# A gated FFN on one core: sixteen of its 22 up chunks by seven products of block sums, and the down projection cut into six parts

## The chip, the cores and the metric

The kernel runs on one core of one Trainium2 chip. Its engines work side by side, each through its own queue of instructions in a fixed order: PE (matmuls, with PEld for the loading of weights), ACT (activations and copies), DVE (elementwise work on vectors), POOL (GpSimd) and SP, which issues most DMAs. The metric is the time of one execution on the device, in microseconds (us), as the median of several runs.

## The reference

An encoder of two layers on 512 tokens of width 1024. Layer 0 mixes tokens by gated linear attention in both directions, layer 1 by grouped-query softmax attention; both end in the same kind of FFN, which is what changes here:

```
def conv_ffn(h, w_up, w_conv, b_conv, w_down):
    u = h @ w_up                                  # 512 x 1024 by 1024 x 5632
    u = conv over 3 neighbouring tokens of each feature + b_conv
    val, gate = jnp.split(u, 2, axis=-1)          # 2816 features each
    return (jax.nn.silu(gate) * val) @ w_down     # 512 x 2816 by 2816 x 1024

x = x + conv_ffn(rmsnorm(x, norm_ffn[i]), ...)
```

All inputs are float32.

## The kernel before

Features lie on the 128 partitions and the 512 tokens along the free axis (S = 512, P = 128). x is held as eight tiles x[0] to x[7] of 128 x 512.

**Precision by two pieces.** A matmul operand is split into a high part, rounded to fp32r by ACT (L143), and a low part, the rest, by DVE (L144). A product of two such operands is three matmuls: high by high, high by low, low by high (mm3, L268 to L272). Each matmul has weights of 128 x 128 and streams 512 columns into one bank of PSUM.

**Weights.** The class Weights holds a list of things to make, in the order in which they are used. half() makes what is wanted, if it isn't there yet, and one piece more. A piece is half of a raw tile: 1 MB comes by DMA on SP's queue into one of two raw buffers, and each half (128 x 1024) becomes a pair wh, wl with three buffers each. For some attention weights the low part is made by ACT (L124) and an accumulating DMA on POOL's queue (L133) instead of DVE.

**Norm.** Norm.chunk(c) makes high and low parts of the weighted x[c] (tiles xhl, L235, L240) and sums squares (L244, L248). The 1/rms of each token is applied late: tokens() forms it by small matmuls (L256), DVE, a power on POOL (L204) and a copy (L260); rows() transposes it to a row layout R (L211, L266). The up products are multiplied by R as they leave PSUM (L605).

**FFN.** For each of 22 chunks of 128 features (FC = 22) the loop runs two tiles, t = 0 the value and t = 1 the gate, of 8 x 3 matmuls (feature_tile) in banks of the tags "acc" (three) and "s" (two). Then for each: times R (L605, DVE), the middle tap with bias (L607, ACT), the two outer taps (L608, L609, DVE); silu on the gate (L611, ACT), the product (L612, DVE), and its high and low parts gu (L614 ACT, L615 DVE), which stay in SBUF. When all 22 chunks are done, the down projection runs for each of eight output tiles over all 22 chunks, 66 matmuls into one bank, and adds the bank to x[c] (L633). In layer 0 Norm.chunk(c) of the next norm follows at once; in layer 1 the tile goes to the output (L637), and the last tile is handled in two halves of 256 columns (L640, L641).

**Order.** The program is written as a sequence of tiles and instructions. When it is built, a planner orders each engine's queue from that sequence and from what it expects to be ready, and puts in the waits for data and for buffers that are still in use. On the chip each queue runs in that order.

## Time and profile before

| | us |
|---|---|
| time of a run: median of 3 | 1134.56 |
| lowest and highest | 1133.87, 1135.52 |
| span of the profiled execution, from the first to the last instruction | 1132.5 |
| PE, DVE, ACT, POOL busy in the profiled execution | 1124.2, 683.7, 481.2, 86.2 |
| first FFN, about 237 to 532 us: PE, DVE busy | 295.0, 191.3 |
| attention, about 532 to 773 us: PE, DVE busy | 239.8, 145.2 |
| second FFN with the tail, about 773 to 1133 us: PE, DVE busy | 355.8, 202.4 |

The time of the profiled execution itself is known only as its span; the runs' median is 2.1 us above it, for what lies around the first and the last instruction. In the rows below, L12 is line 12 of the kernel before; a group reads "line engine operation out<-in, shapes xcount | busy us, mean ns | idle time before it and what ended it". Records of matmuls overlap, since they are pipelined: the distance from one start to the next is the time that a matmul costs in a row of them.

### The profile page before, as it was taken

The numbers are of one execution on the slowest core, as the hardware profiler recorded it, in microseconds if no ns is written. First come the engines' busy times: TensorE is split into PE (matmuls) and PEld (weight loads), VectorE is DVE, ScalarE is ACT, GpSimd is POOL, SyncE is SP. The second block draws the span as 40 slices with busy tenths as digits, with TensorE's granted clock in tenths as the row PEclk, the third lists the DMA queues.
The fourth block names the chain that finished last, engine by engine and source line by source line (L and its number), as shares of the span: only waits on it lengthen the run. The fifth ranks groups of instructions, "written<-read, shape, count | busy, mean of one in ns | idle before, by whom it ended". The sixth has DMA issues, their size and how long they took to land. (4 is left out here: it accounts for less than half of the span.)

```text
span 1132.5 us, 13117 instructions
## 1 busy us (share of the span) xinstructions
PE 1124.2 (99%) x5266; PEld 937.4 (83%) x5266; DVE 683.7 (60%) x989; ACT 481.2 (42%) x690; POOL 86.2 (8%) x74
## 2 busy tenths in 40 slices
PE   9999999999999999999999999999999999999998
PEld 7878888888888888888888888888888888888887
DVE  6576654577777777633325688766777677762221
ACT  5555233444444444422234667644444444442210
POOL 0214110000000000000004343000000000000000
PEclk9999999999999999999999999999999999999999
DMA  6322221222323223233247765423232232323320
GB/s 230 121 100 77 75 75 38 75 98 89 112 75 112 95 91 112 76 110 106 81 132 194 182 171 158 150 75 112 75 112 80 107 111 76 111 84 121 130 93 19
DMA packets 24589, 120.06 MB, mean 106 GB/s; under 512 B 2896, under 2 KB 3536, under 8 KB 13008
## 3 DMA queue, kind: packets, MB, share of 16 engines
q1 hardware_dynamic: 17328, 102.29, 26.0%
q0 software_dynamic: 2304, 8.39, 3.9%
q10 hardware_dynamic: 4896, 8.54, 2.1%
q8 instruction: 41, 0.67, 0.2%
q14 instruction: 20, 0.16, 0.0%
HBM read 100.34 MB, written 2.10 MB: 90 GB/s over the span
## 5 line engine op out<-in xcount | busy, mean ns | idle before, releaser
L143 ACT ACTIVATE wh<-raw 128x1024 fp32r<-128x1024 f32 x164 | 172.9, 1055 | 338.0 <-PE up L271 132.8
L144 DVE TENSOR_TENSOR wl<-raw,wh 128x1024 fp32r<-128x1024 f32 x164 | 203.8, 1243 | 142.7 <-ACT wh L143 142.3
L270 PE MATMUL up<-xhl,wh 128*128 128x512 f32 x704 | 274.3, 390 | 0.0
L272 PE MATMUL up<-xhl,wl 128*128 128x512 f32 x704 | 273.9, 389 | 0.0
L271 PE MATMUL up<-xhl,wh 128*128 128x512 f32 x704 | 273.9, 389 | 0.0
L271 PEld LDWEIGHTS up<-xhl,wh 128*128 128x128 f32 x704 | 132.2, 188 | 27.6
L272 PEld LDWEIGHTS up<-xhl,wl 128*128 128x128 f32 x704 | 132.1, 188 | 27.4
L270 PEld LDWEIGHTS up<-xhl,wh 128*128 128x128 f32 x704 | 132.1, 188 | 27.2
L271 PE MATMUL dn<-gu,wh 128*128 128x512 f32 x354 | 137.3, 388 | 0.0
L272 PE MATMUL dn<-gu,wl 128*128 128x512 f32 x354 | 137.3, 388 | 0.0
L270 PE MATMUL dn<-gu,wh 128*128 128x512 f32 x354 | 137.3, 388 | 0.0
L605 DVE TENSOR_TENSOR u<-up,R 128x512 f32<-128x512 f32 x88 | 60.3, 687 | 52.7 <-PE up L272 52.7
L299 PE MATMUL vg<-wh,xhl 128*128 128x512 f32 x256 | 80.1, 391 | 1.5 <-DVE halfneg L188 0.7
L607 ACT ACTIVATE y<-u,cw 128x512 f32<-128x512 f32 x88 | 71.1, 811 | 20.4 <-DVE u L605 20.4
L270 PEld LDWEIGHTS dn<-gu,wh 128*128 128x128 f32 x354 | 66.5, 188 | 13.8
L271 PEld LDWEIGHTS dn<-gu,wh 128*128 128x128 f32 x354 | 66.5, 188 | 13.7
L272 PEld LDWEIGHTS dn<-gu,wl 128*128 128x128 f32 x354 | 66.5, 188 | 13.5
L325 PE MATMUL op<-oT,wh 128*128 128x512 f32 x256 | 71.1, 394 | 0.3 <-DVE oT L710 0.3
L609 DVE SCALAR_TENSOR_TENSOR y<-u,cw,y 128x511 f32<-128x511 f32 x88 | 65.9, 751 | 2.9
L608 DVE SCALAR_TENSOR_TENSOR y<-u,cw,y 128x511 f32<-128x511 f32 x88 | 65.6, 746 | 0.6 <-ACT y L607 0.6
L611 ACT ACTIVATE y<-y 128x512 f32<-128x512 f32 x44 | 27.9, 633 | 87.8 <-DVE y L609 87.8
L299 PEld LDWEIGHTS vg<-wh,xhl 128*128 128x128 f32 x256 | 48.0, 188 | 12.4 <-DVE g L368 1.0
(187 smaller groups left out, 1432.3 us busy)
## 6 DMA issues: line engine op xcount, KB each, us to landing
raw<-in_w_up_dram SPq DMA_DIRECT2D x44, 1024.0 KB, 4.8
raw<-in_w_down_dram SPq DMA_DIRECT2D x22, 1024.0 KB, 4.8
wl<-raw POOLq DMA_DIRECT2D x16, 512.0 KB, 4.8
pr<-p ACTq DMA_DIRECT2D x32, 256.0 KB, 3.1
raw<-in_w_vg_dram SPq DMA_DIRECT2D x6, 1024.0 KB, 4.8
raw<-in_w_akq_dram SPq DMA_DIRECT2D x5, 1024.0 KB, 5.3
raw<-in_w_kq_dram SPq DMA_DIRECT2D x4, 1024.0 KB, 4.7
raw<-in_w_gout_dram SPq DMA_DIRECT2D x4, 1024.0 KB, 4.8
```

The lines of the kernel that those rows point to most:

```text
L143: act.activation(hi[:, sl], r[:, sl], AF.Copy)
L144: dve.tensor_tensor(lo[:, sl], r[:, sl], hi[:, sl].bitcast(F32), ALU.subtract)
L270: mm(ps, wh, mh, start=start, stop=False)
L271: mm(ps, wh, ml, start=False, stop=False)
L272: mm(ps, wl, mh, start=False, stop=stop)
L299: mm(ps[j][:, :width], hl[k][i == 2][:, js[j]], (wl if i == 1 else wh)[:, sl], start=k == 0 and i == 0, stop=k == KC - 1 and i == 2)
L325: mm(pss[ng][n], wt[:, sl], mv, start=k == 0 and i == 0, stop=k == KC - 1 and i == 2)
L605: dve.tensor_tensor(u, ps, norm.R, ALU.mult)
L607: act.activation(y, u, AF.Identity, scale=w(1), bias=w(3))
L608: dve.scalar_tensor_tensor(y[:, 1:], u[:, : S - 1], w(0), y[:, 1:], ALU.mult, ALU.add)
L609: dve.scalar_tensor_tensor(y[:, : S - 1], u[:, 1:], w(2), y[:, : S - 1], ALU.mult, ALU.add)
L611: act.activation(res[1], res[1], AF.Silu)
```

## The change

Chunks 0 to 5 of each layer (PLAIN = 6) stay as they were, in a new function plain(). For chunks 6 to 21 seven() computes the value and the gate tile by a scheme of seven block products. The input is cut into four blocks: 512 features (four k tiles) by 256 tokens (half of the columns). The weights of a chunk are four blocks too: value and gate by the two halves of the 1024 input features. Instead of eight block products (each 4 x 3 matmuls of 256 columns) there are seven, on sums and differences of blocks.

- build() makes the input's forms once for each layer, during the plain chunks 1 and on (STEPS steps after each tile): the normed input h with R already multiplied in (scaled input), the four sums T1 to T4, and high and low parts of the seven forms used. T3 and T4 are combined on POOL, the rest on DVE.
- rowA1, sum12, sum43 and oneA22 make the weights' forms for each chunk: four sums of 512 columns on DVE, and high and low parts of three pieces of 1024 and one of 512.
- seven() uses two banks, X and Y, of 512 columns each, of which every half is a product of its own or a sum of two: A1 by B11 and S12 by T2 in X, S12 by T1 and S43 by T3 in Y, then B21 onto the left half of X, T4 and B22 onto the halves of Y. ACT and DVE take v and the parts of u out in between. The gate's conv taps change sign for these chunks (one pass over them at the end of the GLA stage).
- The down projection runs in six parts (PARTS: 4, 4, 4, 4, 3, 3 chunks). A part's eight tiles of 4 or 3 units (three matmuls each) lie between the products of the following chunks (BESIDE), each with its own bank and its own add into x[c] (finish). The last part runs at the end; its first three tiles begin with all but the last chunk's units. Down weights are loaded in halves of 512 KB.
- The list of things to make follows this order, with up to two pieces ahead in the plain chunks and four in the others (AHEAD). The low parts of the up weights of chunks 0 to 3 (BY_DMA = 4) come by ACT and an accumulating DMA.
- rows() is called after four steps of chunk 0's second tile instead of behind it. Weight pieces share one tag "w" of six buffers and the eight "xhl" buffers; temporaries move to pools that live for one stage.
- In the last chunk and behind it, matmuls keep the order of the program.

The diff, cut to its core:

```diff
+PLAIN = 6
+PARTS = (4, 4, 4, 4, 3, 3)
+TILES = {4: (2, 2, 2, 2), 3: (2, 3, 3)}
+AHEAD = 4
+EARLY = 1
+ROWS_AT = 3
+BY_DMA = 4
+FIRST_DMA = False
+STEPS = 4
+SHARES1 = (0, 2, 3, 3)
...
+        def convert(self, key, r, spare, by_dma):
+            n = r.shape[1]
+            new = lambda n_: pair("xhl", 8, F32R, "x" + n_) if spare else pair("w", 6, F32R, n_)
+            if n == S:
+                t = new("w")
+                hi, lo = t[:, :S], t[:, S:]
+            else:
+                hi, lo = new("wh"), new("wl")
+            act.activation(hi, r, AF.Copy)
+            if by_dma:
                 act.activation(lo, r, AF.Copy, scale=-1.0)
...
+                self.pending.append((lo.bitcast(F32), r))
             else:
...
+                dve.tensor_tensor(lo, r, hi.bitcast(F32), ALU.subtract)
+            self.made[(id(key[0]),) + key[1:] if not isinstance(key[0], str) else key] = (hi, lo)
+        def rowA1(self, key):
+            _, layer, m = key
+            self.convert(key, self.raw[layer, m][:, : 2 * S], m > PLAIN, m == PLAIN and FIRST_DMA)
+        def sum12(self, key):
+            _, layer, m = key
+            r = self.raw[layer, m]
+            e = self.sums[layer, m] = big(F32, "sum") if m <= PLAIN + 1 else pair("w", 6, F32, "sum")
+            dve.tensor_tensor(e[:, :S], r[:, 2 * S : 3 * S], r[:, 3 * S :], ALU.add)
+            dve.tensor_tensor(e[:, S:], e[:, :S], r[:, :S], ALU.add)
+            self.convert(key, e, m > PLAIN, m == PLAIN and FIRST_DMA)
+        def sum43(self, key):
+            _, layer, m = key
+            r, e = self.raw[layer, m], self.sums[layer, m]
+            dve.tensor_tensor(r[:, S : 2 * S], r[:, S : 2 * S], e[:, S:], ALU.add)
+            dve.tensor_tensor(r[:, 2 * S : 3 * S], r[:, 2 * S : 3 * S], r[:, :S], ALU.add)
+            self.convert(key, r[:, S : 3 * S], False, False)
+        def oneA22(self, key):
+            _, layer, m = key
+            self.convert(key, self.raw.pop((layer, m))[:, 3 * S :], True, False)
+            del self.sums[layer, m]
...
         def half(self, src, n):
...
+            return self.get((id(src), n // 2, n % 2))
+        def get(self, key):
             self.flush()
             while key not in self.made:
                 self.make(self.todo.pop(0))
...
+            while self.todo and len(self.made) <= self.ahead:
                 self.make(self.todo.pop(0))
             return self.made.pop(key)
...
+    def schedule():
+        beside, m = {}, 0
+        for p, n in enumerate(PARTS):
+            tiles = part_tiles(p - 1) if p else []
+            for share in TILES[n] if p != 1 else SHARES1:
+                beside[m], tiles, m = tiles[:share], tiles[share:], m + 1
+        return beside
+    BESIDE = schedule()
+    def add_ffn(layer):
+        for m in range(PLAIN):
+            W.todo.append((up[layer], m, 0))
+            if m == PLAIN - 1:
+                W.todo.append(("load", layer, PLAIN))
+            W.todo.append((up[layer], m, 1))
+            W.early += part_keys(layer, BESIDE[m])
+            W.todo += part_keys(layer, BESIDE[m])
+        for m in range(PLAIN, FC):
+            if m + 1 < FC:
+                W.todo.append(("load", layer, m + 1))
+            W.todo += [(n, layer, m) for n in ("rowA1", "sum12", "sum43")]
+            W.todo += part_keys(layer, BESIDE[m])
+            W.todo.append(("oneA22", layer, m))
+        W.todo += part_keys(layer, part_tiles(len(PARTS) - 1))
...
+    W.by_dma += [(a, 1) for a in qk_order + [w_av]] + [(w_aout, 2)] + [(a, BY_DMA) for a in up]
...
+        taps = cw.rearrange("p (l t m w) -> p l t m w", l=2, t=2, m=FC)
+        for l in range(2):
+            v_ = taps[:, l, 1, PLAIN:, 0:3]
+            dve.tensor_scalar(v_, v_, -1.0, None, ALU.mult)
...
+        def build():
+            hs = []
+            for i in range(4):
+                t = big(F32, "h")
+                for e in range(2):
+                    c = 2 * i + e
+                    dve.scalar_tensor_tensor(t[:, e * S : (e + 1) * S], x[c], norm.weight(c), norm.R,
+                                             ALU.mult, ALU.mult)
+                hs.append(t.rearrange("p (c s) -> p c s", s=S))
+            q2 = (slice(0, 2), slice(2, 4))
+            blk = lambda i, j: [hs[2 * i + q][:, :, j * H : (j + 1) * H] for q in range(2)]
+            b11, b12, b21, b22 = blk(0, 0), blk(0, 1), blk(1, 0), blk(1, 1)
+            v4 = lambda t: t.rearrange("p (k s) -> p k s", s=H)
+            def pieces(name, srcs):
+                hi, lo = v4(big(F32R, "th")), v4(big(F32R, "tl"))
+                n = 4 // len(srcs)
+                for q, src in enumerate(srcs):
+                    sl = slice(q * n, (q + 1) * n)
+                    act.activation(hi[:, sl], src, AF.Copy)
+                    dve.tensor_tensor(lo[:, sl], src, hi[:, sl].bitcast(F32), ALU.subtract)
+                forms[name] = (hi, lo)
+            def combine(eng, dst, a, b, op):
+                for q in range(2):
+                    eng.tensor_tensor(dst[:, q2[q]], a[q], b[q], op)
...
+            pieces("B11", b11)
+            t1, t2, t3 = (v4(big(F32, "ts")) for _ in range(3))
+            combine(dve, t1, b11, b12, ALU.subtract)
+            combine(dve, t2, b22, halves(t1), ALU.add)
+            pieces("T2", [t2])
+            pieces("T1", [t1])
+            combine(pool, t3, b22, b12, ALU.subtract)
+            combine(pool, t2, halves(t2), b21, ALU.subtract)
+            pieces("B21", b21)
+            pieces("B22", b22)
+            pieces("T3", [t3])
+            pieces("T4", [t2])
...
+        def gated(m, u):
+            y = wide("y")
+            for t in (1, 0):
+                cc = ((layer * 2 + t) * FC + m) * 4
+                w = lambda i: cw[:, cc + i : cc + i + 1]
+                ut, yt = u[:, t * S : (t + 1) * S], y[:, t * S : (t + 1) * S]
+                act.activation(yt, ut, AF.Identity, scale=w(1), bias=w(3))
+                dve.scalar_tensor_tensor(yt[:, 1:], ut[:, : S - 1], w(0), yt[:, 1:], ALU.mult, ALU.add)
+                dve.scalar_tensor_tensor(yt[:, : S - 1], ut[:, 1:], w(2), yt[:, : S - 1], ALU.mult, ALU.add)
+                if t:
+                    act.activation(y[:, S:], y[:, S:], AF.Silu)
+            dve.tensor_tensor(y[:, :S], y[:, :S], y[:, S:], ALU.mult)
+            t = big(F32R, "gu")
+            act.activation(t[:, :S], y[:, :S], AF.Copy)
+            dve.tensor_tensor(t[:, S:], y[:, :S], t[:, :S].bitcast(F32), ALU.subtract)
+            hl.append((t[:, :S], t[:, S:]))
+        def plain(m, part):
+            u = wide("u")
             for t in range(2):
                 ps = bank("s" if t else "acc", "up")
...
+                for k, _ in enumerate(feature_steps(*W.half(up[layer], 2 * m + t), norm.hl, ps)):
+                    if m == 0 and t == 1 and k == ROWS_AT:
+                        norm.rows()
                 if m == 0 and t == 0:
                     norm.tokens()
...
+                elif m > 0:
+                    for _ in range(STEPS):
+                        next(building, None)
+                if m == 0 and t == 1:
+                    dve.tensor_tensor(u[:, :S], first, norm.R, ALU.mult)
+                    dve.tensor_tensor(u[:, S:], ps, norm.R, ALU.mult)
+                elif m > 0:
+                    dve.tensor_tensor(u[:, t * S : (t + 1) * S], ps, norm.R, ALU.mult)
+                first = ps
+            for c, us in BESIDE[m]:
+                down_tile(part - 1, c, us, False)
+            gated(m, u)
...
+        def product(dst, pair_, at, form, start, stop):
+            hi, lo = forms[form]
+            for kk in range(4):
+                sl = slice((at + kk) * P, (at + kk + 1) * P)
+                for i, (w, b) in enumerate(((pair_[0], hi), (pair_[0], lo), (pair_[1], hi))):
+                    mm(dst, w[:, sl], b[:, kk], start=start and kk == 0 and i == 0,
+                       stop=stop and kk == 3 and i == 2, skip_group_check=True)
...
+        def down_tile(p, c, us, last):
             ps = bank("acc", "dn")
...
+            k0 = sum(PARTS[:p])
+            late = []
+            for i, u in enumerate(us):
                 if u % 8 == 0:
...
+                    cur[0] = W.half(down[layer], u // 8)
                 sl = slice((u % 8) * P, (u % 8 + 1) * P)
...
+                if last and nxt is None and c == KC - 1 and i >= len(us) - 2:
+                    late.append((cur[0][0][:, sl], cur[0][1][:, sl], *hl[k0 + i]))
                     continue
...
+                mm3(ps, cur[0][0][:, sl], cur[0][1][:, sl], *hl[k0 + i], i == 0, i == len(us) - 1)
...
+        def finish(c, ps, last):
+            dve.tensor_tensor(x[c], x[c], ps, ALU.add)
+            if last and nxt is not None:
+                nxt.chunk(c)
+            elif last:
+                sync.dma_start(out[c * P : (c + 1) * P, :], x[c])
+        def seven(m, part):
+            X = bank("s", "X")
+            a1 = W.get(("rowA1", layer, m))
+            product(X[:, :H], a1, 0, "B11", True, False)
+            s12 = W.get(("sum12", layer, m))
+            product(X[:, H:], s12, 4, "T2", False, True)
+            v = stage[-1].tile([P, H], F32, tag="v", bufs=2, name=nm("v"))
+            act.activation(v, X[:, :H], AF.Copy)
+            dve.tensor_tensor(v, v, X[:, H:], ALU.subtract)
+            Y = bank("pt", "Y")
+            product(Y[:, :H], s12, 0, "T1", True, False)
+            s43 = W.get(("sum43", layer, m))
+            product(Y[:, H:], s43, 4, "T3", False, False)
+            u = wide("u")
+            dve.tensor_tensor(u[:, 3 * H :], v, Y[:, :H], ALU.add)
+            dve.tensor_tensor(u[:, 3 * H :], u[:, 3 * H :], Y[:, H:], ALU.add)
+            product(X[:, :H], a1, 4, "B21", False, True)
+            act.activation(u[:, :H], X[:, :H], AF.Copy)
+            tiles = list(BESIDE[m])
+            pinned[0] = m == FC - 1
+            for c, us in tiles[: EARLY if m == FC - 1 else None]:
+                down_tile(part - 1, c, us, False)
+            a22 = W.get(("oneA22", layer, m))
+            product(Y[:, H:], a22, 0, "T4", False, True)
+            product(Y[:, :H], s43, 0, "B22", False, True)
+            for c, us in tiles[EARLY if m == FC - 1 else FC :]:
+                down_tile(part - 1, c, us, False)
+            with tc.high_priority() if m == FC - 1 else ExitStack():
+                dve.tensor_tensor(u[:, H : 3 * H].rearrange("p (t s) -> p t s", s=H),
+                                  v.rearrange("p (t s) -> p t s", t=1).to_broadcast([P, 2, H]),
+                                  Y.rearrange("p (t s) -> p t s", s=H), ALU.add)
+                gated(m, u)
...
+        early = [(c, us, bank("acc", "dn")) for c, us in tiles[:3]]
+        for late in (False, True):
+            for c, us, ps in early:
+                for i, u in enumerate(us):
+                    if (i == len(us) - 1) != late:
+                        continue
+                    if u // 8 not in ends_:
+                        ends_[u // 8] = W.half(down[layer], u // 8)
+                    wh, wl = ends_[u // 8]
+                    sl = slice((u % 8) * P, (u % 8 + 1) * P)
+                    mm3(ps, wh[:, sl], wl[:, sl], *hl[k0 + i], i == 0, late)
+                if late:
+                    finish(c, ps, True)
+        cur[0] = ends_[tiles[3][1][0] // 8]
+        for c, us in tiles[3:]:
+            down_tile(len(PARTS) - 1, c, us, True)
```

## What the change does to the time: the prediction

> **What bounds the kernel now.** I read the page first (busy times, the 40 slices), then the busy time by stretches, then the order of time on PE and on DVE inside the first FFN, and last the waits.
>
> ```profile
> span 1132.5 us, 13117 instructions
> PE 1124.2 (99%) x5266; PEld 937.4 (83%) x5266; DVE 683.7 (60%) x989; ACT 481.2 (42%) x690; POOL 86.2 (8%) x74
> ...
> L270 PE MATMUL up<-xhl,wh 128*128 128x512 f32 x704 | 274.3, 390 | 0.0
> ...
> 250.00:520.00 270.00, 270.00 (x1193) 223.54 (x1192) 180.75 (x227) 113.25 (x142) 0.00 (x0) 1.00 0.28 98
> ...
> 820.00:1090.00 270.00, 270.00 (x1193) 223.58 (x1192) 161.70 (x199) 100.33 (x121) 0.00 (x0) 1.00 0.29 103
> ```
>
> PE is busy in 99% of the span and in all of both FFN stretches (columns of the last two rows: stretch, PE, PEld, DVE, ACT, POOL, granted clock 1.00, DMA share, GB/s). A busy PE may still be a slow one, so I take the pitch, from start to start:
>
> ```profile
> 255.02 0.39 PE L272 MATMUL up<-xhl,wl 128*128 128x512 f32 x1
> ...
> 261.82 0.39 PE L272 MATMUL up<-xhl,wl 128*128 128x512 f32 x1
> ...
> 654.90 0.29 PE L272 MATMUL po<-pth,vl 128*128 128x256 f32 x1
> ...
> 655.98 0.28 PE L272 MATMUL po<-pth,vl 128*128 128x256 f32 x1
> ```
>
> In the first pair 30 matmuls of 512 columns lie in 6.80 us: 0.2267 us each, no gap. In the second pair nine of 256 columns, each with weights of its own, lie in 1.08 us: 0.120 us each. So PE runs at its own pace in the FFN, and whatever takes matmul time away shortens the run, as long as the rest keeps up. DVE is the next engine: 180.75 of 270 us, ACT 113.25.
>
> **The change on PE.** Chunks 6 to 21 of both layers (32 chunks) replace two tiles of 8 x 3 matmuls of 512 columns by seven products of 4 x 3 of 256. Before: 48 x 0.2267 = 10.88 us. After: 84 x 0.120 = 10.08 us. That is 0.80 us a chunk, **25.6 us in all**; the 36 extra matmuls eat much of the eighth that the arithmetic saves (10.88 / 8 = 1.36). The down projection keeps its 22 x 8 x 3 matmuls of 512 columns and only moves. So the bound from PE alone is 25.6 us less.
>
> The Trainium skill, "TensorE: Matmul & The Clock Gate", section "Wait — 56ns, not 53.3ns?", gives N / 2.4 + 2.5 ns as the warm pitch, 215.8 and 109.2 ns here; by it the saving would be 48 x 0.2158 - 84 x 0.1092 = 1.19 us a chunk, an estimate of 38 us. The trace has 226.7 and 120 ns, so I go by the trace.
>
> **The change on DVE.** Its rows overlap a little, so I count pitches too.
>
> ```profile
> 303.98 0.69 DVE L615 TENSOR_TENSOR gu<-y,gu 128x512 fp32r<-128x512 f32 x1 [0.70 <-ACT gu L614]
> 304.59 0.68 DVE L605 TENSOR_TENSOR u<-up,R 128x512 f32<-128x512 f32 x1
> 305.19 1.22 DVE L144 TENSOR_TENSOR wl<-raw,wh 128x1024 fp32r<-128x1024 f32 x1
> 306.32 0.75 DVE L608 SCALAR_TENSOR_TENSOR y<-u,cw,y 128x511 f32<-128x511 f32 x1
> 307.10 0.75 DVE L609 SCALAR_TENSOR_TENSOR y<-u,cw,y 128x511 f32<-128x511 f32 x1
> ...
> 310.03 1.23 DVE L144 TENSOR_TENSOR wl<-raw,wh 128x1024 fp32r<-128x1024 f32 x1 [0.17 <-ACT wh L143]
> ...
> 697.38 1.40 DVE L683 SCALAR_TENSOR_TENSOR rt<-B,prm,rope 128x512 f32<-128x512 f32 x2
> 698.70 0.68 DVE L820 TENSOR_TENSOR ptl<-pt,pth 128x512 fp32r<-128x512 f32 x1
> ```
>
> (Columns: start, us, engine, line, operation, shapes, and in brackets an idle time before it.) Of shapes that matter the groups say, with count, busy us, mean ns, idle before:
>
> ```profile
> L443 DVE TENSOR_TENSOR ga<-ga,t 128x256 f32<-128x256 f32 x8 | 3.3, 418 | 0.0
> L527 ACT ACTIVATE sa<-kv 128x256 f32<-128x256 f32 x8 | 3.1, 384 | 8.3 <-PE kv L526 8.3
> L143 ACT ACTIVATE wh<-raw 128x1024 fp32r<-128x1024 f32 x164 | 172.9, 1055 | 338.0 <-PE up L271 132.8 <-PE dn L271 127.5 <-PE op L325 34.1
> L607 ACT ACTIVATE y<-u,cw 128x512 f32<-128x512 f32 x88 | 71.1, 811 | 20.4 <-DVE u L605 20.4
> L611 ACT ACTIVATE y<-y 128x512 f32<-128x512 f32 x44 | 27.9, 633 | 87.8 <-DVE y L609 87.8
> ```
>
> Pitches: two tensors of 512 elements 0.60 us (303.98 to 304.59 to 305.19), of 1024 1.13 (to 306.32), a scalar_tensor_tensor 0.78 when the next needs its result (to 307.10), else 0.66 (two in 1.32, to 698.70). For 256 elements I take the row's 0.418 less the 0.08 by which the others overlap: 0.34.
>
> A seven-product chunk then asks of DVE: four block sums of 512, 2.4; three low parts of 1024 and one of 512, 3 x 1.13 + 0.60 = 4.0; v and the two adds of 256, 1.0; the last sum from PSUM, 0.60; four conv taps, 2 x (0.78 + 0.66) = 2.9; product and low part of gu, 1.2. That is 12.1. In the usual case (two tiles of four units beside it) come one low part of the down weights, 1.13, and two adds into x, 1.2. **DVE 14.4 us, and about 14.6 with the dependent adds; PE 10.08 + 8 x 3 x 0.2267 = 15.52 us.** Before, the same work took PE 10.88 + 5.44 = 16.32 and DVE 2 x 1.13 + 2 x 0.60 + 2.9 + 1.2 + 1.13, about 8.7. So DVE goes from 53% to 94% of PE's time, and is what can spoil the saving. ACT: 3 x 1.055 + 0.633 for high parts, 2 x 0.384, 2 x 0.811, 2 x 0.633, and 1.055 for the down half: 8.5 us, no bound. POOL has no sums here. Each chunk loads 1.5 MB in 15.5 us, 101 GB/s, about what the stretch rows show now (98 and 103).
>
> Can a fixed queue keep PE fed at 94%? The nearest rows:
>
> ```profile
> 244.00:255.00 11.00, 11.00 (x50) 9.09 (x49) 10.24 (x15) 5.21 (x8) 0.00 (x0) 1.00 0.25 84
> ...
> 700.00:710.00 10.00, 9.88 (x67) 8.47 (x66) 9.71 (x22) 6.66 (x15) 6.20 (x5) 1.00 0.49 131
> ...
> 720.00:730.00 10.00, 9.33 (x55) 7.37 (x54) 7.19 (x19) 6.15 (x13) 0.88 (x1) 1.00 0.53 147
> ...
> DVE y L612 <- ACT y L611: 32.5, 43, 0.8
> DVE gu L615 <- ACT gu L614: 29.6, 42, 0.8
> ```
>
> With DVE at 93% PE lost nothing, at 97% 1.2%; in the worst stretch of the attention 6.7%, with a DVE at 72%. The stretches that change hold 16 x 10.08 + 144 x 0.68 = 259 us a layer, 518 in all (144 of 176 down units lie there), so the loss is 0 to 35 us. I take **2%, 10 us** (0.3 us a chunk), near the 93 and 97% rows: the weights are prepared four pieces ahead, and that work can fill DVE's gaps.
>
> Where would the loss sit? The product that comes fifth in a chunk (B21) goes back into bank X, and must wait until ACT has copied one half and DVE subtracted the other.
>
> ```profile
> 1127.83 0.28 PE L272 MATMUL dn<-gu,wl 128*128 128x256 f32 x1
> ...
> 1128.55 0.28 PE L272 MATMUL dn<-gu,wl 128*128 128x256 f32 x1
> ...
> 1128.86 0.75 DVE L640 TENSOR_TENSOR x<-x,dn 128x256 f32<-128x256 f32 x2 [13.70 <-PE dn L272]
> ```
>
> The left half of that bank was complete at 1128.11, yet DVE read it at 1128.86, once the right half was done at 1128.83: the program orders accesses by whole banks. The Trainium skill, "PSUM — Partial Sum Buffer", section "PSUM bank collisions raise a hardware error", demands that, and the trace agrees with the 0.75 us. In the new chunk the two products on Y lie between, 24 x 0.120 = 2.88 us, against 0.384 + 0.418 = 0.80 us of work. So 2 us are spare: one 1.13 us low part ahead of it in DVE's queue costs nothing, two or a queue that lags cost PE the difference.
>
> **The rest of the change.** Building the forms: eight scalar_tensor_tensor, four adds of 512 and seven low parts, 8 x 0.66 + 4 x 0.60 + 7 x 1.15 = 15.7 us of DVE over chunks 1 to 3; those chunks lose 8 x 1.13 of low parts for chunks 0 to 3, which go to ACT and a DMA (four chunks: 4 x 5.3 + 15.7 = 37 of 43.5 us of PE). Hidden, though chunk 2 alone is over its 10.88 and leans on the banks ahead.
>
> The rows of R are wanted after four steps of the second tile, 12 x 0.2267 = 2.72 us after the token sums:
>
> ```profile
> 236.83 0.95 PE L256 MATMUL ms<-ones,sq 128*128 128x1 f32 x8
> ...
> 238.05 1.01 POOL L204 TENSOR_TENSOR rtok<-rtok,halfneg 128x4 f32<-128x4 f32 x1 [49.02 <-DVE rtok L200]
> ...
> 239.09 0.17 DVE L260 COPY rtok<-rtok 128x4 f32<-128x4 f32 x1 [1.12 <-POOL rtok L204]
> ...
> wl<-raw POOLq DMA_DIRECT2D x16, 512.0 KB, 4.8
> ...
> cw<-in_conv_dram SPq DMA_DIRECT2D x1, 176.0 KB, 6.7
> ```
>
> The chain from 236.83 to 239.26 is 2.4 us, so it just fits; POOL's queue now also holds the accumulating DMAs of the first weights, each waiting for ACT, so up to 1 us twice. The sign flips of the taps wait on DVE for a 6.7 us load: nothing if planned late, up to 4 us of a DVE queue with PE's evictions behind it. At the end of the first FFN eight finished tiles come 2.04 us apart (9 x 0.2267) where 14.96 us lay between (66 x 0.2267); each costs DVE 0.60 + 0.66 + 0.60 = 1.9, so DVE may end 4 to 5 us behind, of which the first seven steps of the next projection (21 x 0.2267 = 4.8 us) hide most: 0 to 2. The tail keeps its form. Together 0 to 8 us; I take 2, since most are covered.
>
> **Sum.** Against the profiled execution, span 1132.5 (the median of the runs, 1134.56, is 2.1 us above it and goes with the same steps): -25.6 + 10 + 2 = -13.6, span 1119, time **1121 us**. Bounds: -25.6 + 0 + 0 gives 1109, -25.6 + 35 + 8 gives 1152.
>
> **Rivals.** (1) PE loses next to nothing: 1108 to 1113. For it speaks the 93% row with PE at 11.00 of 11.00; against it that this held for one 11 us stretch, not for 16 chunks in a row. (2) **Slower: DVE becomes the bound.** Its order is fixed, so if the round trips to ACT stay unfilled it pays 14.6 + 0.76 + 0.70 (the two wait rows, each over its count) + 0.4 for v behind ACT's copy + 0.5 for high parts that come late (three times the 0.17 of row 310.03) = 17.0 us a chunk, over the 16.32 that PE took before: 32 x 0.65 = 21 us slower, and with the 2 us of edges 1157. It decides once DVE stands idle 1.7 us a chunk (16.32 - 14.6). For it: in each chunk of before DVE does wait for ACT's silu and gu. Against: there it had nothing else ready; now it has. (3) DVE's period comes out near 16.2, and saving and loss cancel: 1128 to 1137. (4) The 256-column products don't hold 0.120 us with 84 in a row; at 0.13 the saving is gone (84 x 0.13 = 10.9). The 96 products of the attention's values, up to the first matmul behind them, speak against it:
>
> ```profile
> 616.55 0.28 PE L299 MATMUL av<-wh,xhl 128*128 128x256 f32 x1
> ...
> 628.07 0.40 PE L270 MATMUL s<-k,q 128*128 128x512 f32 x1
> ```
>
> They take 11.52 us, again 0.120 each, so I leave this inside (3).
>
> **How the numbers follow.** Forecast, 1113 to 1128: 0.48. Rival 1: 0.17. Rival 3: 0.12, half of it within 0.2%, which is what a measurement here can tell from no change. Rival 2 and other slower ends, above 1137: 0.23, of which 0.13 above 1145. Faster 0.48 + 0.17 + 0.04 = 0.69, same 0.06, slower 0.25. The range of 8 in 10 runs from 1108, below which only 0.05 lies, to 1145.
>
> **What will show it.** Right: pitches of 0.120 in the products; in the stretch of chunks 6 to 21 DVE at 92 to 96% and ACT near 55%; PE waits of a few tenths of a us a chunk, ahead of the fifth product (released by DVE's v) or of weights' low parts; chunk periods of 15.5 to 16.0 us. Wrong: periods above 16.3 with DVE full or waiting for ACT, or long waits of PE on a DMA, which I don't expect. It is also wrong if PE loses over 4 us at the ends of the stages.

## The result and the profile after

| | before | after |
|---|---|---|
| median of the runs, us | 1135.04 (4 runs) | 1126.28 (4 runs) |
| lowest and highest | 1133.87, 1135.52 | 1125.06, 1127.20 |
| span of the profiled execution | 1132.5 | 1124.6 |

The ratio is 0.9925, with a 95% interval of 0.9911 to 0.9939: 8.8 us faster, where 13.6 were forecast. The time lies within the range and within the forecast's own 1113 to 1128. But two of the forecast's terms were wrong, in opposite directions. Where the time went shows in three views. First the page of the kernel after (span, then busy us and instructions of each engine):

```profile
span 1124.6 us, 16137 instructions
...
PE 1104.3 (98%) x6418; PEld 971.2 (86%) x6418; DVE 887.7 (79%) x1355; ACT 576.1 (51%) x854; POOL 121.2 (11%) x98
```

PE went from 1124.2 us busy to 1104.3, DVE from 683.7 to 887.7. The busy time by stretches of the kernel after comes next (stretch, PE, PEld, DVE, ACT, POOL, granted clock, DMA share, GB/s). The stretches are the plain chunks and the first products, chunks 6 to 21, and the end of the first FFN; then the first two of these for the second FFN:

```profile
247.00:326.00 79.00, 74.65 (x364) 62.35 (x364) 74.62 (x97) 43.20 (x56) 11.38 (x7) 1.00 0.47 137
326.00:560.00 234.00, 234.00 (x1616) 218.87 (x1615) 212.74 (x310) 117.15 (x162) 0.00 (x0) 1.00 0.32 108
560.00:575.00 15.00, 14.25 (x73) 11.61 (x73) 10.98 (x15) 5.61 (x8) 0.00 (x0) 1.00 0.01 1
763.00:843.00 80.00, 74.68 (x326) 60.78 (x325) 67.85 (x91) 45.89 (x59) 17.09 (x11) 0.98 0.50 140
843.00:1100.00 257.00, 257.00 (x1766) 239.97 (x1765) 230.41 (x334) 127.28 (x175) 0.00 (x0) 1.00 0.29 97
```

The rows of chunks 6 to 21, where all the doubt of the prediction lay, show PE full, with DVE at 91% and 90%. The rows of the plain chunks, which were to cost nothing, show PE short by 4.35 and 5.32 us. The waits of PE name what it lacked there (us in total, times, longest):

```profile
PE up L85 <- DVE wl L220: 4.8, 2, 2.7
PE dn L85 <- ACT wh L166: 2.5, 2, 1.8
PE dn L85 <- DVE wl L171: 1.6, 1, 1.6
PE dn L85 <- DVE x L841: 1.3, 2, 0.7
```

L220 is the low part of an up weight of a plain chunk, L166 and L171 are the two parts of the first down weights, and L841 is the add of a finished down tile into x. A full PE can still run slowly, so I also summed over all pairs of neighbouring starts what lies above 0.2267 us for a matmul of 512 columns, 0.120 for 256, and so on. This is my own count from the starts, in us; "three edits" is the best version, further down:

| stage | before | after | three edits |
|---|---|---|---|
| up to the first FFN | 26.4 | 25.8 | 28.0 |
| first FFN, plain chunks to first products | 0 | 5.3 | 0.3 |
| first FFN, chunks 6 to 21 | 0 | 0 | 0 |
| first FFN, end | 0 | 1.4 | 1.4 |
| attention | 9.2 | 11.0 | 11.0 |
| second FFN, plain chunks to first products | 0 | 7.9 | 0.3 |
| second FFN, chunks 6 to 21 | 0 | 0 | 0 |
| second FFN, end | 0 | 1.3 | 1.4 |
| all, with the small rest | 35.6 | 53.2 | 42.8 |

The 28.0 of the three edits ahead of the first FFN belongs to the start of that execution and to no edit: from 4.4 to 9.7 us PE made 13 matmuls there, against 22 in the kernel after.

The balance closes: the products save 25.6 us of pitch, PE loses 17.6 more than before, and 8.0 remain, against 7.9 between the spans. So the question for the experiments is what those 17 us are, and whether DVE at 91% is near an edge.

### The profile page after: what moved, and what is told of

It reads as the page before. It is cut to its first block, busy times and chain, and to the rows that moved or that the text cites. A ratio compares the mean times of both kernels' runs of the same rounds, so it can differ in the third digit from the quotient of the medians.

```text
span 1124.6 us, 16137 instructions
## 1 busy us (share of the span) xinstructions
PE 1104.3 (98%) x6418; PEld 971.2 (86%) x6418; DVE 887.7 (79%) x1355; ACT 576.1 (51%) x854; POOL 121.2 (11%) x98
## 4 chain that ended last, share of the span: by engine, by line
PE 78%; DVE 12%; issue 4%; ACT 3%; DMA 2%; POOL 1%; ACTq 0%; DVEq 0%; SPq 0%; POOLq 0%
PE dn L85 19%; PE Y L85 16%; PE X L85 12%; PE op L85 8%; PE vg L85 5%; PE k L85 2%; PE q L85 2%; PE up L85 2%; PE po L85 2%; PE s L85 2%; PE o L85 2%; PE A L85 1%; PE B L85 1%; DVE y L776 1%; DVE y L777 1%
## 5 line engine op out<-in xcount | busy, mean ns | idle before, releaser
L85 PE MATMUL up<-xhl,wh 128*128 128x512 f32 x384 | 118.8, 390 | 0.0
L85 PE MATMUL X<-th,xwh 128*128 128x256 f32 x360 | 101.9, 283 | 0.0
L85 PE MATMUL X<-th,xwl 128*128 128x256 f32 x360 | 101.9, 283 | 0.0
L85 PE MATMUL X<-tl,xwh 128*128 128x256 f32 x360 | 101.9, 283 | 0.0
L166 ACT ACTIVATE wh<-raw 128x1024 fp32r<-128x1024 f32 x66 | 69.8, 1057 | 57.4 <-PE op L85 14.5
L841 DVE TENSOR_TENSOR x<-x,dn 128x512 f32<-128x512 f32 x95 | 64.7, 684 | 31.6 <-PE dn L85 31.4
L85 PEld LDWEIGHTS up<-xhl,wh 128*128 128x128 f32 x384 | 71.8, 188 | 14.8
L166 ACT ACTIVATE wh<-draw 128x1024 fp32r<-128x1024 f32 x44 | 46.7, 1061 | 71.9 <-PE dn L85 35.7
L85 PE MATMUL up<-xhl,wl 128*128 128x512 f32 x192 | 75.0, 391 | 4.8 <-DVE wl L220 4.8
L85 PE MATMUL Y<-th,wh 128*128 128x256 f32 x264 | 74.7, 283 | 0.0
L85 PE MATMUL Y<-tl,wh 128*128 128x256 f32 x264 | 74.7, 283 | 0.0
L85 PE MATMUL Y<-th,wl 128*128 128x256 f32 x264 | 74.7, 283 | 0.0
L219 ACT ACTIVATE wh<-raw 128x1024 fp32r<-128x1024 f32 x40 | 42.0, 1053 | 59.9 <-PE op L85 18.8
L220 DVE TENSOR_TENSOR wl<-raw,wh 128x1024 fp32r<-128x1024 f32 x40 | 53.9, 1351 | 23.4 <-ACT wh L219 19.7
```

Source lines behind the costliest of these rows:

```text
L85: i = pe.matmul(*a, **k)
L166: act.activation(hi, r, AF.Copy)
L219: act.activation(hi[:, sl], r[:, sl], AF.Copy)
L220: dve.tensor_tensor(lo[:, sl], r[:, sl], hi[:, sl].bitcast(F32), ALU.subtract)
L841: dve.tensor_tensor(x[c], x[c], ps, ALU.add)
```

## The experiments

All ratios are to the kernel before, with their 95% intervals. Diffs are against the kernel after.

### The sums T3 and T4 on DVE

POOL combines T3 and T4 while DVE works on the plain chunks. The DVE timeline of the kernel after in the second FFN has (start, us, line, operation):

```profile
803.31 2.49 DVE L735 TENSOR_TENSOR tl<-h,th 128x512 fp32r<-128x512 f32 x4
805.72 3.49 DVE L777 SCALAR_TENSOR_TENSOR y<-u,cw,y 128x511 f32<-128x511 f32 x2
809.13 2.28 DVE L220 TENSOR_TENSOR wl<-raw,wh 128x1024 fp32r<-128x1024 f32 x1
811.33 1.78 DVE L780 TENSOR_TENSOR y<-y 128x512 f32<-128x512 f32 x1
```

Its POOL timeline there has:

```profile
801.68 6.97 POOL L740 TENSOR_TENSOR ts<-ts,h 128x512 f32<-128x512 f32 x2 [6.19 <-DVE tl L735]
808.61 3.94 POOL L740 TENSOR_TENSOR ts<-h,h 128x512 f32<-128x512 f32 x2
```

While POOL's four sums run, a pair of taps takes 3.49 us, a low part 2.28 and a product 1.78. The edit:

```diff
-            combine(pool, t3, b22, b12, ALU.subtract)
-            combine(pool, t2, halves(t2), b21, ALU.subtract)
+            combine(dve, t3, b22, b12, ALU.subtract)
+            combine(dve, t2, halves(t2), b21, ALU.subtract)
```

> The input forms T3 and T4 are combined on DVE instead of POOL; all else is as in the changed kernel (1126.3 us). Contention theory (DVE and POOL slow each other while POOL forms these sums; rows of 0.7 to 1.2 us stand at 1.8 to 2.3): those rows come back to their usual length, the wait of PE for the low part of chunk 4 in the second FFN (2.9 us) falls below 1 us, total 3 to 5 us less. Load theory (DVE simply has too much to do in chunks 1 to 4): DVE gets 2 x 4 x 0.6 = 4.8 us more work, the waits of PE in the plain chunks grow, total 2 to 5 us more. Queue theory (the down weights are late because their loads stand in SP's queue): no change within 1 us.

Measured: 1124.41 us, 0.9907 [0.9890, 0.9924]. The DVE timeline of this kernel at the same place:

```profile
803.87 1.29 DVE L740 TENSOR_TENSOR ts<-h,h 128x512 f32<-128x512 f32 x2
805.08 1.29 DVE L740 TENSOR_TENSOR ts<-ts,h 128x512 f32<-128x512 f32 x2
806.28 2.49 DVE L735 TENSOR_TENSOR tl<-h,th 128x512 fp32r<-128x512 f32 x4
808.69 1.41 DVE L777 SCALAR_TENSOR_TENSOR y<-u,cw,y 128x511 f32<-128x511 f32 x2
810.01 1.22 DVE L220 TENSOR_TENSOR wl<-raw,wh 128x1024 fp32r<-128x1024 f32 x1
811.15 0.69 DVE L780 TENSOR_TENSOR y<-y 128x512 f32<-128x512 f32 x1
```

The same work takes 1.41, 1.22 and 0.69 us, so POOL's sums were what slowed DVE. Yet by the medians the time fell only 1.9 us, and the intervals overlap. PE's waits in this kernel say why:

```profile
PE dn L85 <- ACT wh L166: 6.4, 2, 4.5
PE up L85 <- ACT wh L219: 1.8, 1, 1.8
```

The wait for L220 is gone, but the wait for the first down weights grew from 4.1 us (L166 and L171) to 6.4. PE now comes to them sooner, and they come no sooner. The queue of SP in this kernel shows the issue of three such loads, and the ACT timeline the use of the one that is wanted first:

```profile
289.02 0.33 SPq L179 DMA_DIRECT2D raw<-in_w_up_dram  x1
293.05 2.10 SPq L142 DMA_DIRECT2D draw<-in_w_down_dram  x3
```

```profile
301.14 1.06 ACT L166 ACTIVATE wh<-draw 128x1024 fp32r<-128x1024 f32 x1 [4.46 <-DMA draw<-in_w_down_dram]
```

The loads are issued from 293.05 on and ACT can use the first down weights only at 301.14, while PE stands. The wait left in the second FFN, for L219, is a high part on ACT: it stands in ACT's queue behind a silu whose taps wait in DVE's queue behind the building of the forms.

### Low parts of six chunks by DMA

```diff
-BY_DMA = 4
+BY_DMA = 6
```

> The low parts of chunks 4 and 5 are also made by ACT and an accumulating DMA, which takes 4 x 1.13 = 4.5 us a layer from DVE. Load theory: the waits of PE for low parts of chunk 4 (2.3 and 2.9 us) vanish and those ahead of the first down tiles (2.6 and 3 us) mostly too, total 8 to 12 us less. Contention theory: the first waits vanish, the slowed rows stay; 4 to 6 us less. Queue theory: only the first waits vanish, those at the down tiles stay; 4 to 5 us less.

Measured: 1127.12 us, 0.9926 [0.9911, 0.9940], no gain, which none of the theories had. PE's waits in this kernel:

```profile
PE up L85 <- DMA wl<-raw: 9.6, 3, 4.3
```

DVE is relieved and the wait for the down weights is gone, but low parts made this way now arrive late by ACT, POOL's queue and an accumulating DMA (6.1 us from issue to landing around 280 us, by its list of DMA issues). One late supplier took the place of another.

### The early down loads on ACT's queue

```diff
-                sync.dma_start(t, src[i][:, h * 2 * S : (h + 1) * 2 * S])
+                (act if key in self.early else sync).dma_start(t, src[i][:, h * 2 * S : (h + 1) * 2 * S])
```

> The loads of the first down weights, which run beside chunk 5, are issued from ACT's queue instead of SP's, where they stand behind the load of chunk 7 that waits for a raw buffer. Queue theory: the waits ahead of the first down tiles (0.9 and 1.9 us in the first FFN, 2.1 and 1.0 with some 2 us at half clock behind it in the second) vanish, 5 to 8 us less. Load theory and contention theory: the weights are late on DVE anyway, change within 1.5 us.

Measured: 1130.96 us, 0.9960 [0.9946, 0.9975], worse. The issue came to stand at 297.08 in ACT's order, later than on SP's queue in the kernel after, and the waits for L166 grew to 7.4 us. SP's queue in the kernel after:

```profile
281.37 10.52 SPq L179 DMA_DIRECT2D raw<-in_w_up_dram  x2
291.94 4.34 SPq L142 DMA_DIRECT2D draw<-in_w_down_dram  x3
```

The second load of L179 is issued only at 291.57, when a low part (L220) on DVE has given a raw buffer back, and the first down load comes right behind it at 291.94. Its own buffer had been free since 278.4. The experiment doesn't separate the theories: it made the load later, not earlier. That a later load costs time fits with the load being what PE waits for.

### More work for DVE in chunks 6 to 21

The first block sum of each chunk's weights is formed twice in one kernel and four times in another, into the same place; nothing else changes. One more costs DVE about 0.6 us a chunk, three more 1.8.

```diff
             dve.tensor_tensor(e[:, :S], r[:, 2 * S : 3 * S], r[:, 3 * S :], ALU.add)
+            dve.tensor_tensor(e[:, :S], r[:, 2 * S : 3 * S], r[:, 3 * S :], ALU.add)
```

> The first block sum of the weights is done twice in each of the 32 chunks: 0.60 us more of DVE a chunk, which goes from 91 to about 95% in chunks 6 to 21. If DVE has the room that its rows show: within 2 us of the changed kernel (1126.3). If PE was about to be held up by a DVE so full, as the prediction priced it (2% at 94%): 5 to 10 us more, with waits of PE in chunks 6 to 21. If DVE were the bound already: 32 x 0.6 = 19 us more.

> The first block sum of the weights is done four times in each of the 32 chunks: 1.8 us more of DVE a chunk. DVE's own time in chunks 6 to 21, 91% of PE's in the changed kernel, becomes 14.1 + 1.8 = 15.9 us against 15.5 of PE. If PE is held up only when DVE is really full: 0.4 us a chunk and a little for hand-overs, 12 to 20 us more than the changed kernel (1126.3), with waits of PE spread over these chunks. If a full DVE costs more than its own excess (round trips to ACT that can't be filled): 30 us and more. No change would say that DVE's pitches were read wrongly.

Measured: one more, 1126.85 us, 0.9924 [0.9908, 0.9940], no loss; three more, 1143.57 us, 1.0073 [1.0050, 1.0095], which is 17.3 us slower than the kernel after. The stretch of the chunks with one more:

```profile
326.00:560.00 234.00, 234.00 (x1618) 218.96 (x1617) 221.22 (x324) 116.83 (x162) 0.00 (x0) 1.00 0.33 111
```

With three more, by stretches, the second row being the last chunk and the end:

```profile
326.00:560.00 234.00, 232.98 (x1597) 216.48 (x1597) 231.33 (x347) 112.44 (x158) 0.00 (x0) 1.00 0.29 102
560.00:575.00 15.00, 11.72 (x65) 10.53 (x65) 9.86 (x14) 6.04 (x9) 0.00 (x0) 0.89 0.40 141
```

At 94.5% DVE costs PE nothing. At 98.9% PE loses 3 us in the middle of each layer's chunks by my count. Another 5 us or so a layer go in the last chunk, where PE's order is fixed and a product waits for DVE to read bank Y. The profile has this as a wait of PE on L865, 6.5 us in two pieces, with a lower clock behind it (0.89). The time was as expected, but most of the loss lies in that last chunk and not spread over all of them. So the edge lies where DVE is full, and the kernel after stands about 1.4 us a chunk below it (9% of 15.5 us).

### The sums on DVE, and three building steps a tile

With T3 and T4 on DVE, build() goes three steps after each tile instead of four, so that the building of the forms is spread over more plain chunks.

```diff
-STEPS = 4
+STEPS = 3
```

> T3 and T4 on DVE as in the first run (1124.4 us), and the forms built in three steps after each tile instead of four, so that they reach into chunk 4. Load theory (a burst in chunk 2 is what makes the parts of chunk 4 late): the wait ahead of chunk 4 in the second FFN (2.0 us) vanishes, 2 to 3 us less than the first run. Against it: the work only moves to chunk 4, whose own low parts then come late; within 1 us. The waits ahead of the first down tiles (4.6 and 2.1 us) stay in both.

Measured: 1129.01 us, 0.9943 [0.9927, 0.9958], 2.7 above the kernel after, which neither expectation had. PE's waits:

```profile
PE dn L85 <- ACT wh L166: 9.0, 2, 4.7
```

Every wait for up weights (L219, L220) is gone, and the wait for the down weights has grown to 4.84 and 4.44 us by my count, each with matmuls at half rate behind it, which cost some 2 us more. The two causes lie in a row: whoever cures the first alone meets the second sooner.

### The first down weights loaded a chunk earlier

The list asks for the raw down weights of chunk 5 one chunk ahead, and they come into two free buffers of their own. So they stand neither in the buffers of the forms nor in SP's queue behind a load that waits for an old buffer: in the first FFN that was the raw load above, in the second a down load into an "xhl" buffer (issued at 828.33, the wanted one behind it at 828.70).

```diff
...
+        def dload(self, key):
+            src, i, h = key[2]
+            t = [tmp("sq", "draw") for _ in range(2)]
+            for q in range(2):
+                o = (2 * h + q) * S
+                sync.dma_start(t[q], src[i][:, o : o + S])
+            self.draw[id(src), i, h] = t
...
+            if m == PLAIN - 2:
+                W.todo += [("dload", layer, k) for k in part_keys(layer, BESIDE[PLAIN - 1])]
```

> The raw down weights for the tiles beside chunk 5 are loaded in chunk 4 into two free temporaries, so that neither SP's queue nor the buffers of the forms hold them back; POOL sums and four steps as in the changed kernel. If their load is what makes the first down tiles wait: these waits (2.6 and 3 us, and some 2 us at half clock) vanish, 4 to 7 us less than the changed kernel (1126.3). If DVE's backlog does it: the wait stays within 1 us, since the low part comes as late as before.

Measured: 1122.48 us, 0.9885 [0.9868, 0.9902], 3.8 us better, a little under what was expected. PE's waits (L237 is the old L220):

```profile
PE up L85 <- DVE wl L237: 4.8, 2, 2.7
```

The down waits are gone and the up waits stand as before, to the tenth. Together with the runs that have the sums on DVE this shows both causes, each by its own cure. The edit changes the time of the request, its place in SP's queue and its buffers at once; which of them does it wasn't tried apart.

### The cures together

T3 and T4 on DVE with the early load; then with STEPS = 3 as well (three edits); then also with the tiles of the short parts shared out as (2, 2, 4), so that four down tiles instead of three lie beside the last of them (all four).

> T3 and T4 on DVE and the early load, but four steps as in the changed kernel. If both stalls are independent, the wait ahead of chunk 4 in the second FFN (2.0 us in the run with DVE sums alone) is all that stays in the plain chunks: 1117 to 1118 us. If three steps matter for more than that: above 1119.

> The run before it (1117.3 us) without the new deal of tiles beside chunks 19 to 21: T3 and T4 on DVE, three steps, early load of the down weights. If the three edits take all waits out of the plain chunks and the new deal made the ends worse (2.2 us a layer against 1.1): 1115 us, 2 us less than that run.

> T3 and T4 on DVE, three steps, the early load of the down weights, and the tiles beside chunks 19 to 21 dealt 2, 2, 4 instead of 2, 3, 3, which puts 2 us more of matmuls behind the last chunk's products. If the stalls at the edges are all that the change lost: the waits at the end of both FFNs (1.3 us each) vanish too, PE's idle time in the plain chunks falls below 3 us a layer, 1113 to 1117 us. If one of them only moves: 1119 to 1123.

| | us | ratio |
|---|---|---|
| sums on DVE, early load | 1116.38 | 0.9829 [0.9809, 0.9849] |
| three edits | 1115.43 | 0.9815 [0.9794, 0.9835] |
| all four | 1117.25 | 0.9837 [0.9820, 0.9854] |

By the medians the first cure alone gave 1.9 us and the second 3.8, both together 9.9; by the spans of the profiled executions 2.8, 4.9 and 8.8. So the surplus of both over their sum is between 1 and 4 us. With the first cure alone, part of its gain was paid back at the down weights (6.4 us of waits against 4.1); with the second alone the up waits stayed as they were. With three edits the transition of the first FFN is full and the chunks stay so:

```profile
270.00:310.00 40.00, 39.96 (x196) 33.72 (x195) 39.76 (x58) 23.44 (x33) 0.00 (x0) 1.00 0.32 106
326.00:556.00 230.00, 230.00 (x1587) 215.09 (x1587) 210.46 (x308) 113.97 (x158) 0.00 (x0) 1.00 0.32 109
```

Here DVE is at 99% for 40 us and PE loses almost nothing, since the work is spread so that what PE needs next comes first. Three edits and the first pair can't be told apart by their times; the third edit shows only in the wait of 1.8 us for L236 (the old L219), which the pair still has and the three edits don't. The fourth edit gained nothing: the waits for the add into x at the ends of the FFNs grew from 1.4 us in the profile of three edits to

```profile
PE dn L85 <- DVE x L860: 3.7, 4, 1.2
```

L860 is L841 of the kernel after.

### An earlier order at the end

With the three edits, EARLY goes from 1 to 2.

```diff
-EARLY = 1
+EARLY = 2
```

> The three edits, and in the last chunk two down tiles ahead of its last two products instead of one (EARLY = 2). If the waits at the ends (1.1 us a layer) are for banks that DVE frees late, because its adds into x stand behind the gated work of the last chunk: they shrink, 1113 to 1115 us. If they are for gu of the last chunk: they grow by up to 2.7 us a layer, 1117 to 1120.

Measured: 1117.67 us, 0.9842 [0.9823, 0.9861], 2.2 above the three edits, whose slowest run (1116.41) is below its fastest (1117.45). The wait at the end of each FFN is now 2.5 us. The DVE timeline at the first:

```profile
564.12 1.41 DVE L796 SCALAR_TENSOR_TENSOR y<-u,cw,y 128x511 f32<-128x511 f32 x2
565.45 1.22 DVE L180 TENSOR_TENSOR wl<-draw,wh 128x1024 fp32r<-128x1024 f32 x1
566.59 0.68 DVE L799 TENSOR_TENSOR y<-y 128x512 f32<-128x512 f32 x1
567.19 0.68 DVE L860 TENSOR_TENSOR x<-x,dn 128x512 f32<-128x512 f32 x1
567.97 0.69 DVE L802 TENSOR_TENSOR gu<-y,gu 128x512 fp32r<-128x512 f32 x1
```

PE resumes at 567.92, when the add into x (L860) has given a bank back. The add stands in DVE's queue behind the last chunk's taps, a low part and the product, though nothing in its own data holds it so long. The time is the one that was expected if PE waited for the last gu, but the profile names the bank, and PE resumes before the low part of gu (L802) begins. That moving the add would help is only argued: the low part of the last gu comes right behind it, and PE might wait for that instead.

### The parts without the products

All 22 chunks are plain (PLAIN = 22, BY_DMA = 0), without the forms and without the flipped taps; the down projection keeps its six parts. It computes the same by the old products.

> No chunk by seven products (all 22 plain, no forms, no sign change, no low parts by DMA for the up weights); only the down projection in six parts. PE's work is that of the kernel before, so if parts cost only the waits at the ends: 1135 to 1138 us. Less than 1133 would mean that the parts bring something by themselves, and that the products bring less than the 25.6 us of their matmuls; above 1140 that interleaving has a price of its own.

Measured: 1138.46 us (12 runs), 1.0027 [1.0016, 1.0038]. The parts alone gain nothing and cost 3.3 us; in its profile most of that is at the start of the attention, where PE waits for a weight's low part by DMA:

```profile
PE A L85 <- DMA wl<-raw: 2.2, 1, 2.2
```

Against the three edits, which have the parts and the products, this gives the worth of the products by itself: 1138.46 - 1115.43 = 23.0 us. By the spans it is 22.8, and the three edits lose 2.9 us more over the pitch (42.8 against 39.9), so 25.7 us come from the products themselves; 25.6 were worked out.

The products without the parts weren't tried: the buffers of 22 gu and of the forms don't fit beside each other.

## Why the prediction was right, and where it was not

**The term of PE was right.** 84 x 0.120 against 48 x 0.2267 gave 25.6 us; the runs give 25.7. The pitch of 0.120 held with 84 products in a row, so rival 4 is out. The figure of the Trainium skill's page "TensorE: Matmul & The Clock Gate", section "Wait — 56ns, not 53.3ns?", by which the estimate was 38 us, is not borne out: the pitches were 0.2267 and 0.120 us.

**The budget of DVE was right, slightly high.** 94% was worked out, with 92 to 96% as the sign of being right; 91 and 90% were measured. For ACT it was 55% and 50%.

**The price of a full DVE was wrong.** "I take 2%, 10 us, near the 93 and 97% rows" is the step. PE lost nothing in 32 chunks, as rival 1 had it, and 0.6 us a chunk more (94.5%) still cost nothing. The rows that I drew on, 97% with a loss of 1.2% and 72% with 6.7%, were from the attention, whose work hangs together otherwise; that its losses come from the order of dependent work and not from how full DVE is, is an argument and wasn't tried. What the runs show is that such rows don't carry over to chunks whose weights are prepared four pieces ahead. The wait of the fifth product for its bank never showed: the 2 us to spare were enough. DVE can become the bound, as rival 2 had it, but not by idling for ACT: three more sums a chunk, 1.8 us, made the kernel 17.3 us slower than the kernel after, with DVE 98.9% busy in the chunks.

**The edges were the step that failed the other way.** "Together 0 to 8 us; I take 2, since most are covered" met 15.9 us in the two FFNs (5.3, 1.4, 7.9, 1.3), and by the prediction's own test, "over 4 us at the ends of the stages", its reasons were wrong here. Only 2.7 us of this lie at the ends; 13.2 lie in the plain chunks, whose extra work was called hidden. Of its parts:

- "Hidden, though chunk 2 alone is over" was said of building the forms. I compared sums over four chunks (37 of 43.5 us) where what counts is each chunk. By stretches of about a chunk (columns as above) the kernel after has DVE at 11.00 of 11 us in two stretches in a row, and the low part that PE needs next stands in that queue:

```profile
258.00:269.00 11.00, 11.00 (x50) 9.09 (x49) 10.03 (x12) 6.29 (x9) 3.42 (x3) 1.00 0.77 185
269.00:280.00 11.00, 11.00 (x51) 9.09 (x50) 11.00 (x13) 5.62 (x9) 6.25 (x2) 1.00 0.29 95
280.00:291.00 11.00, 8.90 (x40) 6.98 (x39) 11.00 (x15) 7.96 (x11) 0.00 (x0) 1.00 0.27 95
```

- I gave no price to T3 and T4 on POOL. They made work on DVE slower by 2.08 + 1.06 + 1.09 = 4.2 us in the second FFN (the rows above: 3.49, 2.28 and 1.78 against 1.41, 1.22 and 0.69). Done on DVE itself they take 1.21 and 1.20 by the starts, 2.4 in all. The Trainium skill, "SBUF — State Buffer", section "Who interferes with whom", states that a DVE instruction with two inputs in SBUF contends with a GpSimd instruction that reads SBUF. By its section "Summary: rules for kernel authors" the later one is blocked until the first is done. The slow rows agree with both; four low parts in 2.49 us while POOL's long pair is shown running may be the side that went first.
- The load of the first down weights wasn't in the sum at all. I counted its bytes and not its issue, which stands in SP's queue behind a load that waits for a buffer of the old order (291.94 in the first FFN, though its own buffer was free at 278.4). Long waits of PE on a DMA were named as a sign of being wrong; in the second FFN this is one, by way of ACT. Loaded early from buffers of its own it was worth 3.8 us alone, and some 8 once the sums were off POOL (1124.41 to 1116.38).
- One of PE's waits in the kernel after, that for the second FFN's down weights, brought 3.4 us at half rate behind it, some 1.7 us of loss, which no step had.
- The chain of rows() and the flips of the taps cost nothing that shows, as taken. The end of the first FFN cost 1.4 us, within its 0 to 2; the tail, which "keeps its form", cost 1.3 too, since its last chunk and adds meet in DVE's queue like those of the first.

Attention lost 1.8 us more than before; I didn't look for its cause.

**The sum.** -25.6 + 10 + 2 was forecast, -25.6 + 0 + 17.6 measured. Two errors of 10 and 16 us partly cancelled: that the total came so near was luck, for reasons that were half wrong. With the stalls of the plain chunks cured, as in the three edits, the kernel runs at 1115.43. By the spans that is 18.4 us under the kernel before: 25.6 less the 7.2 that it still loses over before by my count (42.8 - 35.6).

## What to carry to other kernels

Work out the budget of the helping engines for the transition between stages chunk by chunk, with the issue and the buffer of each load, and not only for the steady state: here 32 full chunks at 91% cost nothing, and the few plain chunks ahead of them cost 13 us. When a stall is cured and the time hardly moves, look for the next one right behind it before giving the cure up; two cures of 1.9 and 3.8 us were worth 9.9 together by the medians. Keep sums off POOL while DVE is what PE waits for. Ask for the first piece of a new stream ahead of loads that wait for older buffers, and into buffers that nothing older holds.

## What the hardware showed beside that

**A short wait can halve the matmul rate behind it.** The PE timeline of the kernel with the sums on DVE and the early load, in the second FFN (in brackets the idle time and who ended it):

```profile
803.70 0.61 PE L85 MATMUL up<-xhl,wh 128*128 128x512 f32 x2
806.14 0.51 PE L85 MATMUL up<-xhl,wh 128*128 128x512 f32 x1 [1.82 <-ACT wh L236]
806.48 0.46 PE L85 MATMUL up<-xhl,wl 128*128 128x512 f32 x1
806.74 1.06 PE L85 MATMUL up<-xhl,wh 128*128 128x512 f32 x2
807.59 0.63 PE L85 MATMUL up<-xhl,wl 128*128 128x512 f32 x1
808.02 1.06 PE L85 MATMUL up<-xhl,wh 128*128 128x512 f32 x2
```

The stretches there, with the granted clock in the column ahead of the DMA share:

```profile
806.70:809.30 2.60, 2.60 (x8) 2.00 (x6) 2.60 (x5) 2.45 (x4) 0.00 (x0) 0.50 0.00 0
```

One wait, 1.98 us above the pitch from start to start (1.82 idle), is followed, 0.6 us after work resumes, by 3.4 us at a clock of 0.50, of which the row shows 2.6: three matmuls from 806.74 to 808.02 at 0.427 us each. The kernel after shows the same behind the waits that end at 834.87 and 836.89: a clock of 0.50 from 837.2 to 840.6. The Trainium skill, "TensorE: Matmul & The Clock Gate", section "What's actually happening", puts the fall to half rate after an idle window of about 3.4 us. Here a wait of 2 us sufficed. In the kernel with the early load alone one of 2.28 us (above the pitch) was followed by a lower clock and one of 2.84 us was not:

```profile
292.00:295.00 3.00, 3.00 (x10) 2.39 (x9) 3.00 (x5) 1.53 (x3) 0.00 (x0) 0.62 0.70 208
...
811.00:814.00 3.00, 3.00 (x15) 2.45 (x14) 3.00 (x4) 1.67 (x3) 0.75 (x1) 1.00 0.00 0
```

In the kernel after, a wait of 2.27 us at the place of the first had no lower clock behind it. So the length by itself doesn't decide it; what does stays open. With the slow matmuls behind it, a wait costs up to twice its row.

**POOL seems to pay too.** The group of T4's sums in the kernel after (its count, busy us and mean ns ahead of the idle time):

```profile
L740 POOL TENSOR_TENSOR ts<-ts,h 128x512 f32<-128x512 f32 x4 | 13.2, 3321 | 11.6 <-DVE tl L735 11.6
```

The nearest group of the kernel before, of the same shape:

```profile
L427 POOL TENSOR_TENSOR gm<-gm,ga 128x512 f32<-128x512 f32 x8 | 10.4, 1295 | 51.2 <-ACT ga L426 30.2 <-DVE gm L424 15.0 <-DVE wl L144 6.0
```

3.3 us against 1.3: it looks as if both engines lose while they work side by side. That is argued only, since POOL never ran these sums with DVE at rest.
